# Four small transposes moved from TensorE to VectorE squares and a round trip through HBM

## The chip, the cores and the metric

The kernel runs on one core of a Trainium2 chip. The metric is the device time of one execution in microseconds (us). Before the change it is 1434.01 us, the median of three runs (1433.89 to 1434.04).

The core has a matrix engine (TensorE, PE in the views; PEld is its loading of the stationary operand), a vector engine (VectorE, DVE), a scalar engine (ScalarE, ACT), GpSimd (POOL) and a sync engine (SP), which here only issues transfers. Each engine takes its instructions in the order of its own list and waits, where an operand isn't ready, with everything behind it. SBUF is the on-chip memory of 128 partitions, PSUM holds TensorE's results, HBM is the memory off the core.

## What is computed

Two layers of a gated block with two branches on 512 tokens of width 1024, all in float32. From the reference, cut:

```python
proj = rmsnorm(x, norm1_g[i]) @ w_in[i]
u_pool, q, k, v, g_a, g_b = jnp.split(proj, splits, axis=-1)
q = apply_partial_rotary(rmsnorm(q, q_norm_g[i]), cos, sin)   # 4 heads x 2 parts x 128
k = apply_partial_rotary(rmsnorm(k, k_norm_g[i]), cos, sin)
...
sc = jnp.einsum('bhcqd,bhckd->bhcqk', qi, k) * scale
p = jax.nn.softmax(jnp.where(mask, sc, neg), axis=-1)
a = p[:, :, 0] - lam * p[:, :, 1]
o = jnp.einsum('bhqk,bhkv->bhqv', a, v)
o = rmsnorm(o, subln_g[i]) * (1.0 - lam_init)
merged = jax.nn.sigmoid(g_a) * pool_out + jax.nn.sigmoid(g_b) * attn_out
x = x + merged @ w_out[i]
gate, up = jnp.split(rmsnorm(x, norm2_g[i]) @ w_ffn_in[i], 2, axis=-1)
x = x + (jax.nn.silu(gate) * up) @ w_ffn_out[i]
```

The attention mask lets a block of 128 queries see itself and the blocks before it, so block t has (t + 1) x 128 columns of probabilities.

## The kernel before

**Products.** Every float32 operand is split into a high and a low part (`split`: ScalarE casts the high part, VectorE subtracts for the low one), and a product is three matmuls: high x high, high x low, low x high (lines 279 to 281, and 291 to 294 in the feed-forward part). Weights come in pieces of 512 KB (`piece`): a load on SP's queue into `raw` (7 buffers), then the split into `whi` and `wlo` (6 buffers each). Products are accumulated in PSUM: three buffers `mm`, two `sc`, two `tr` and one `oy`.

**One head** (`attention(j, ...)`, four per layer, heads 3, 2, 1, 0 in this order, with blocks t = 0 to 3 of 128 tokens):

- For each t one product of 8 weight rows gives q and k of the head, 512 columns. ScalarE squares them (line 618), VectorE and GpSimd form the scale r (310, 311), VectorE scales (622) and rotates (`rotate`, 418 to 423) into `qn`.
- `turn(t, qn)`: four TensorE transposes of 128x128 into a `tr` buffer, then the split into `qh` and `ql`.
- `scores(t)`: two products into `sc`, mask, maximum, exponential (560), the two probabilities combined into `pr` (563 to 566).
- `turn_prob(t, pr)`: t + 1 transposes into `tr`, then the split into `ah` and `al`.
- `weighted(t, ah, al)`: the product with v into `oy`, normed and gated into `mt` (588 to 591).
- `turn_out(t, m)`: two transposes, and a copy into `mj` (599).

`merged(j, ...)` later computes the pooled branch of the head with four long products and two short ones and adds `mj`. `project_out` multiplies by w_out. The feed-forward part follows. Layer 0's first head (`at_start`) works on data that was loaded as the kernel began.

**The order of the work.** The program keeps a count of issued matmul columns (`clock`). `later(delay, what)` puts a step in a heap, due `delay` columns from now; before each group of three matmuls `run_due` issues the steps that are due. So QK_WAIT is the number of columns that TensorE is given between the q and k product and their transposes, SCORE_WAIT between those and the scores, PROB_WAIT between scores and the transposes of the probabilities, AV_WAIT between those and the product with v, MERGE_WAIT between that and `turn_out`. `need` runs steps of the heap early where a later part wants them. A scheduler then orders each engine's list by this order and by its own estimate of when operands are ready; each tag of buffers is shared in turn by the tiles that name it (`qn` has three buffers).

Of the kernel before, what the change touches and what calls it, by code (L numbers as in the profile page):

```python
# [43 lines left out]

HIDDEN_AT = {0: "u", 2: "m", 4: "pr", 6: "us", 8: "mj", 10: "u", 12: "m", 14: "pr", 16: "us", 18: "u", 20: "m"}

QK_WAIT, SCORE_WAIT, PROB_WAIT, AV_WAIT, NORM_WAIT, MERGE_WAIT = 20400, 33600, 25200, 11400, 15000, 15000


def weight_plan():  # L50
# [57 lines left out]
def trunk_kernel(  # L108
# [13 lines left out]
    const = ctx.enter_context(tc.tile_pool(name="const", bufs=1))  # L122
    sb = ctx.enter_context(tc.tile_pool(name="sb", bufs=1))
    ps = ctx.enter_context(tc.tile_pool(name="ps", bufs=1, space=PSUM))

    def mm_ps():
        return ps.tile([P, 512], F32, name="mm", tag="mm", bufs=3)
# [171 lines left out]
    def transpose(dst, src):  # L299
        nc.tensor.transpose(dst, src, ident)  # L300
        clock[0] += 2 * P

    def rsqrt_mean(ss, n, width, times=(1.0,), eps=None):

# [120 lines left out]
    def token(t):  # L425
        return slice(t * P, (t + 1) * P)
# [85 lines left out]
            transpose(row[:, token(t)], stats[:, 1, t:t + 1].broadcast_to([P, P]))  # L512
        nc.scalar.copy(rms_row, row)

    later(4 * QK_WAIT, spread_rms)

    for layer in range(L):
        lam_init = 0.8 - 0.6 * math.exp(-0.3 * layer)
# [12 lines left out]
        def attention(j, before, then):  # L531

            if before is not None:
                need(*((layer, before, "s", t) for t in range(NT)))
            qh, ql = pair("q", "qk", 4)
            mj = sb.tile([P, 2, S], F32, name="mj", tag="mj", bufs=2)

            def v_at(v, t):
                return v[:, t // 2, t % 2 * VD:(t % 2 + 1) * VD]

            def turn(t, qn):
                tp = tr_ps()
                for h in range(4):
                    transpose(tp[:, h * P:(h + 1) * P], qn[:, h, :])
                split(qh[:, :, token(t)], ql[:, :, token(t)], tp.rearrange("p (h c) -> p h c", h=4))
                later(SCORE_WAIT, lambda: scores(t))

            def scores(t):
                width = (t + 1) * P
                prob = []  # L550
                st = small("st", 2)
                mx = small("mx", 2)
                for c in range(2):
                    sc = s_ps()
                    product(sc[:, :width], [(
                        (qh[:, c, token(t)], ql[:, c, token(t)]), (qh[:, 2 + c, :width], ql[:, 2 + c, :width]))])
                    nc.vector.memset(sc[:CHUNK, width - CHUNK:width], MASKED)
                    nc.vector.tensor_reduce(mx[:, c:c + 1], sc[:, :width], axis=AX.X, op=ALU.max, negate=True)
                    pr = sb.tile([P, S], F32, name="pr", tag=f"pr{c}", bufs=2)
                    nc.scalar.activation(pr[:, :width], sc[:, :width], AF.Exp, bias=mx[:, c:c + 1], accum_out=st[:, c:c + 1])  # L560
                    prob.append(pr[:, :width])
                rc = small("rc", 2)
                nc.vector.reciprocal(rc, st)
                nc.vector.tensor_mul(rc[:, 1:2], rc[:, 1:2], neglam[layer])
                nc.vector.tensor_scalar_mul(prob[1], prob[1], rc[:, 1:2])
                nc.vector.scalar_tensor_tensor(prob[0], prob[0], rc[:, 0:1], prob[1], op0=ALU.mult, op1=ALU.add)
                later(PROB_WAIT + (4000 if at_start and t == NT - 1 else 0), lambda: turn_prob(t, prob[0]))
                ready.add((layer, j, "s", t))

            def turn_prob(t, pr):  # L570
                tp = tr_ps()
                for k in range(t + 1):
                    transpose(tp[:, token(k)], pr[:, token(k)])
                apart = at_start and t % 2
                ah, al = (sb.tile([P, S], F32R, name="a" + p, tag="u" if apart else "a" + p, bufs=2 if apart else 1) for p in "hl")
                width = (t + 1) * P
                split(ah[:, :width], al[:, :width], tp[:, :width])
                later(AV_WAIT, lambda: weighted(t, ah, al))

            def weighted(t, ah, al):  # L580
                if (layer, j, "v", t) not in ready:
                    later(2400, lambda: weighted(t, ah, al))
                    return
                o = s_ps()[:, :VD] if at_start and t % 2 else o_ps()
                product(o, [((ah[:, token(k)], al[:, token(k)]), (v_at(vh, k), v_at(vl, k))) for k in range(t + 1)])
                ss = small("sso")
                m = sb.tile([P, VD], F32, name="mt", tag="mt", bufs=3)
                nc.scalar.activation(m, o, AF.Square, accum_out=ss)
                r = rsqrt_mean(ss, VD, 1, (1.0 - lam_init,))
                nc.vector.scalar_tensor_tensor(m, o, r, sg[layer], op0=ALU.mult, op1=ALU.mult)  # L590
                nc.vector.scalar_tensor_tensor(m, tb[t // 2][:, t % 2, :], 1.0, m, op0=ALU.add, op1=ALU.mult)
                ready.add((layer, j, "o", t))
                later(MERGE_WAIT, lambda: turn_out(t, m))

            def turn_out(t, m):
                tp = tr_ps()
                for a in range(2):
                    transpose(tp[:, a * P:(a + 1) * P], m[:, a * P:(a + 1) * P])
                nc.scalar.copy(mj[:, :, token(t)], tp[:, :VD].rearrange("p (a c) -> p a c", a=2))
                ready.add((layer, j, "mj", t))  # L600

            at_start = not layer and j == ORDER[0]
            if not at_start:
                w = wblock(KD)
            for t in range(NT):
                if at_start:
                    acc = first_acc[t]
                    first_products(t, steps[2] + steps[3])
                    if not t:
                        token_stats()  # L610
                else:
                    need((f"x{layer}", t))
                    acc = mm_ps()
                    product(acc, list(zip(x_tok(t), w)))
                qn = sb.tile([P, 4, QK], F32, name="qn", tag="qn", bufs=3)
                ss = small("ss4", 4)
                for h in range(4):
                    nc.scalar.activation(qn[:, h, :], acc[:, h * QK:(h + 1) * QK], AF.Square, accum_out=ss[:, h:h + 1])
                r = rsqrt_mean(ss, QK, 4, (QK ** -0.5, 1.0), None if layer else [stats[:, i, t:t + 1] for i in (3, 4)])
                for h in range(4):  # L620
                    g = qkg[layer][:, h // 2 * QK:(h // 2 + 1) * QK]
                    nc.vector.scalar_tensor_tensor(
                        qn[:, h, :], acc[:, h * QK:(h + 1) * QK], r[:, h:h + 1], g, op0=ALU.mult, op1=ALU.mult)
                rotate(qn, t)
                later(17400 + 5700 * t if at_start else QK_WAIT, lambda t=t, qn=qn: turn(t, qn))
                if not t and then is not None:
                    then()
            if before is not None:
                need(*((layer, before, "o", t) for t in range(NT)))
            vh, vl = pair("v", "v", 2)  # L630
            tb = [sb.tile([P, 2, VD], F32, name="tb", tag="tb", bufs=2) for _ in range(2)]
            w = wblock(KD)
            if at_start:
                with tc.issue_after(transfers[-1].ins):
                    for i in range(L):
# [373 lines left out]
```

## Time and profile before

| | |
|---|---|
| median of three runs | 1434.01 us |
| the profiled execution | 1433.82 us, its span 1432.0 us |
| TensorE busy | 1427.0 us, 100% of the span |
| VectorE busy | 990.3 us, 69% |
| ScalarE busy | 687.3 us, 48% |
| TensorE clock granted | 1.00 |
| moved by DMA | 171.97 MB |

The attention parts of the two layers stand at about 30 to 350 us and 735 to 1055 us of the span; the feed-forward parts follow each. A row of instruction groups reads: line, engine, operation, written tile <- read tiles, shapes, count | busy us in total, mean ns of one | idle time of the engine ahead of them and what ended it. Where a view gives three numbers in ns they are the least, the median and the most. A matmul's duration runs from its start to its modelled end; the next one starts before that end.

### The profile page before, as it was taken

What the parts mean: (1) busy time and instruction counts of PE and PEld (TensorE: products, weight loads), DVE (VectorE), ACT (ScalarE), POOL (GpSimd) and SP (SyncE); (2) the same over time, 40 slices, a digit from 0 to 9 for tenths busy, and PEclk for the clock granted to TensorE, in tenths of its full rate; (3) what the DMA queues carried; (4) which work ended last, traced back from release to release, by engine and by line L of the source; (5) the groups of instructions that cost most, each with busy time, mean ns of one, the idle gap of its engine ahead of it and who ended that gap; (6) DMA issues with size and microseconds to landing.
All of it is one profiled execution on the core that took longest, in us unless ns stands there. A gap on an engine that the chain in (4) does not pass through costs nothing.

```text
span 1432.0 us, 21581 instructions
## 1 busy us (share of the span) xinstructions
PE 1427.0 (100%) x8378; PEld 1261.0 (88%) x8378; DVE 990.3 (69%) x1839; ACT 687.3 (48%) x1309; POOL 113.5 (8%) x144
## 2 busy tenths in 40 slices
PE   9999999999999999999999999999999999999999
PEld 7888888888999899989888888888889998999897
DVE  7768677677998548737576686665769975577462
ACT  6544343454667346525354443434547662564350
POOL 1010000100001001000011001001000000010000
PEclk9999999999999999999999999999999999999999
DMA  9212231224268357628331232222323683575361
GB/s 363 97 60 78 93 102 59 89 83 116 74 169 203 115 132 182 187 58 235 105 103 67 62 115 82 74 75 73 123 69 87 169 227 93 141 183 162 88 148 59
DMA packets 49494, 171.97 MB, mean 120 GB/s; under 512 B 5616, under 2 KB 6512, under 8 KB 49392
## 3 DMA queue, kind: packets, MB, share of 16 engines
q1 hardware_dynamic: 39456, 137.02, 28.9%
q0 software_dynamic: 8640, 31.46, 12.4%
q10 hardware_dynamic: 1296, 2.11, 0.5%
q8 instruction: 66, 1.08, 0.3%
q14 instruction: 36, 0.29, 0.1%
HBM read 168.47 MB, written 2.10 MB: 119 GB/s over the span
## 4 chain that ended last, share of the span: by engine, by line
PE 99%; DMA 0%; DVE 0%; ACT 0%; issue 0%
PE mm L279 20%; PE mm L281 20%; PE mm L280 20%; PE mm L293 6%; PE mm L294 6%; PE mm L291 6%; PE sc L291 3%; PE sc L294 3%; PE sc L293 3%; PE tr L300 3%; PE tr L294 1%; PE tr L293 1%; PE tr L291 1%; PE sc L281 1%; PE sc L280 1%; PE sc L279 1%
## 5 line engine op out<-in xcount | busy, mean ns | idle before, releaser
L195 ACT CAST whi<-raw 128x1024 fp32r<-128x1024 f32 (+1 forms) x225 | 234.4, 1048 | 207.6 <-issue 119.0
L196 DVE TENSOR_TENSOR wlo<-raw,whi 128x1024 fp32r<-128x1024 f32 (+1 forms) x225 | 271.6, 1214 | 81.9 <-ACT whi L195 79.0
L279 PE MATMUL mm<-whi,xh 128*128 128x512 f32 x480 | 192.4, 401 | 0.0
L281 PE MATMUL mm<-whi,xl 128*128 128x512 f32 x480 | 187.7, 391 | 0.0
L280 PE MATMUL mm<-wlo,xh 128*128 128x512 f32 x480 | 187.3, 390 | 0.0
L722 DVE TENSOR_TENSOR res<-mm,res 128x512 f32<-128x512 f32 (+1 forms) x97 | 65.8, 682 | 116.0 <-PE mm L281 116.0
L281 PE MATMUL mm<-whi,fl 128*128 128x512 f32 (+1 forms) x358 | 138.5, 387 | 0.0
L279 PE MATMUL mm<-whi,fh 128*128 128x512 f32 (+1 forms) x358 | 138.3, 387 | 0.0
L280 PE MATMUL mm<-wlo,fh 128*128 128x512 f32 (+1 forms) x358 | 138.2, 387 | 0.0
L311 POOL TENSOR_TENSOR r<-r,mhalf 128x1 f32<-128x1 f32 (+1 forms) x76 | 59.1, 778 | 633.3 <-DVE r L310 568.8
L281 PEld LDWEIGHTS mm<-whi,xl 128*128 128x128 f32 x480 | 90.1, 188 | 19.6
L279 PEld LDWEIGHTS mm<-whi,xh 128*128 128x128 f32 x480 | 90.3, 188 | 16.8
L280 PEld LDWEIGHTS mm<-wlo,xh 128*128 128x128 f32 x480 | 90.4, 188 | 16.3
L279 PE MATMUL mm<-xh,whi 128*128 128x512 f32 x256 | 102.1, 399 | 0.0
L235 POOL DMA_DIRECT2D wlo<-in_wts x60 | 52.6, 877 | 612.7 <-ACT wlo L234 271.0
L281 PE MATMUL mm<-xh,wlo 128*128 128x512 f32 x256 | 99.9, 390 | 0.0
L280 PE MATMUL mm<-xl,whi 128*128 128x512 f32 x256 | 99.8, 390 | 0.0
L293 PE MATMUL mm<-xql,whi 128*128 128x256 f32 x352 | 99.7, 283 | 0.0
L294 PE MATMUL mm<-xqh,wlo 128*128 128x256 f32 x352 | 99.6, 283 | 0.0
L291 PE MATMUL mm<-xqh,whi 128*128 128x256 f32 x352 | 99.6, 283 | 0.0
L291 PE MATMUL sc<-xqh,whi 128*128 128x256 f32 x320 | 90.7, 283 | 0.0
L291 PE MATMUL mm<-xrh,whi 128*128 128x256 f32 x320 | 90.6, 283 | 0.0
(235 smaller groups left out, 3533.0 us busy)
## 6 DMA issues: line engine op xcount, KB each, us to landing
raw<-in_wts SPq DMA_DIRECT2D x244, 512.0 KB, 4.3
wlo<-in_wts POOLq DMA_DIRECT2D x60, 512.0 KB, 7.7
xr<-in_x_t SPq DMA_DIRECT2D x4, 512.0 KB, 7.2
res<-in_x SPq DMA_DIRECT2D x4, 512.0 KB, 9.3
pwr<-in_pool_w ACTq DMA_DIRECT2D x8, 256.0 KB, 2.7
out<-res SPq DMA_DIRECT2D x7, 256.0 KB, 2.0
g<-in_gains SPq DMA_DIRECT2D x6, 256.0 KB, 3.2
hg<-in_rows SPq DMA_DIRECT2D x4, 128.0 KB, 6.8
```

The costliest lines, as they stand in the source:

```text
L195: ins = nc.scalar.copy(hi, src)
L196: nc.vector.tensor_sub(lo, src, hi.bitcast(F32))
L235: nc.gpsimd.dma_start(lo.rearrange("p a b -> p (a b)"), wts[piece_no], accum_op=ALU.add)
L279: nc.tensor.matmul(acc, lhsT=ah, rhs=bh, start=i == 0, stop=False)
L280: nc.tensor.matmul(acc, lhsT=ah, rhs=bl, start=False, stop=False)
L281: nc.tensor.matmul(acc, lhsT=al, rhs=bh, start=False, stop=i == n - 1)
L291: nc.tensor.matmul(acc[:, i, :], lhsT=ah, rhs=bh, start=start and not i and not k, stop=False, skip_group_check=True)
L293: nc.tensor.matmul(acc[:, i, :], lhsT=ah, rhs=bl, start=False, stop=False, skip_group_check=True)
L294: last = nc.tensor.matmul(acc[:, i, :], lhsT=al, rhs=bh, start=False, stop=i == 1 and k == 3, skip_group_check=True)
L300: nc.tensor.transpose(dst, src, ident)
L311: nc.gpsimd.tensor_tensor(r, r, mhalf[:, :width], op=ALU.pow)
L722: added = nc.vector.tensor_add(res[t][:, cs], here, res[t][:, cs])
```

## The change

For all heads but the first of layer 0, q, k and the probabilities are no longer transposed by TensorE. A new function `turned` has VectorE transpose each 32x32 square of the tile in place of its column of squares, writes the result to a buffer in HBM and reads it back in four transfers, one for each group of 32 partitions, which put each square into its place. The splits into `qh`, `ql`, `ah`, `al` then read SBUF (`near`) instead of PSUM. The heads' outputs go the same way, except for the first head of layer 0 and the last head of each layer (`near_end`). The delays of these steps get new values: QK_AWAY + SCORE_AWAY equals QK_WAIT + SCORE_WAIT, PROB_AWAY is 6800 columns more than PROB_WAIT, MERGE_AWAY 9000 more than MERGE_WAIT. The buffers `near` share the tags `qn`, `pr0`/`pr1` and `mt`.

```diff
+QK_AWAY, SCORE_AWAY, PROB_AWAY, MERGE_AWAY = 28000, 26000, 32000, 24000
...
+    hbm = ctx.enter_context(tc.tile_pool(name="hbm", bufs=1, space=bass.MemoryType.DRAM))
...
+    def turned(src, n, tag, bufs):
+
+        near = sb.tile([P, n * P], F32, name="near", tag=tag, bufs=bufs)
+        away = hbm.tile([P, n * P], F32, name="away", tag="away", bufs=8)
+        nc.vector.transpose(near.rearrange("p (c k j) -> p k c j", c=4, k=n), src.rearrange("p (k c i) -> p k c i", k=n, c=4))
+        nc.sync.dma_start(away, near)
+        for c in range(4):
+            nc.sync.dma_start(
+                near[32 * c:32 * (c + 1), :].rearrange("i (q r) -> i q r", q=4),
+                away.rearrange("(q i) (c r) -> c i q r", q=4, c=4)[c])
+        return near.rearrange("p (q k j) -> p k q j", q=4, k=n)
...
             def turn(t, qn):
-                tp = tr_ps()
-                for h in range(4):
-                    transpose(tp[:, h * P:(h + 1) * P], qn[:, h, :])
-                split(qh[:, :, token(t)], ql[:, :, token(t)], tp.rearrange("p (h c) -> p h c", h=4))
-                later(SCORE_WAIT, lambda: scores(t))
+                if at_start:
...
+                else:
+                    split(squares_of(qh[:, :, token(t)]), squares_of(ql[:, :, token(t)]), qn)
+                later(SCORE_WAIT if at_start else SCORE_AWAY, lambda: scores(t))
...
+                if at_start:
+                    later(PROB_WAIT + (4000 if t == NT - 1 else 0), lambda: turn_prob(t, prob[0]))
+                else:
+                    near = turned(prob[0], t + 1, f"pr{t % 2}", 2)
+                    later(PROB_AWAY, lambda: turn_prob(t, near))
...
-                later(MERGE_WAIT, lambda: turn_out(t, m))
+                if near_end:
+                    later(MERGE_WAIT, lambda: turn_out(t, m))
+                else:
+                    near = turned(m, 2, "mt", 3)
+                    later(MERGE_AWAY, lambda: turn_out(t, near))
...
             at_start = not layer and j == ORDER[0]
+            near_end = at_start or j == ORDER[-1]
...
-                later(17400 + 5700 * t if at_start else QK_WAIT, lambda t=t, qn=qn: turn(t, qn))
+                if not at_start:
+                    qn = turned(qn.rearrange("p h c -> p (h c)"), 4, "qn", 3)
+                later(17400 + 5700 * t if at_start else QK_AWAY, lambda t=t, qn=qn: turn(t, qn))
```

How the change moves the lists of the engines is shown at two places. The first is SP's list in layer 0's attention. Before, behind the loads of x into `res`, one row of 48 weight loads (`raw<-in_wts`) goes on to the feed-forward part:

```order
L209 DMA raw<-in_wts 128x1024 x48
```

After, the same weight loads stand between stores (`away<-near`) and loads (`near<-away`) of the round trips; this is a stretch in the third head, where outputs of the second (128x256), then q and k (128x512) and the first probabilities (128x128) are sent:

```order
L311 DMA away<-near 128x256
L212 DMA raw<-in_wts 128x1024 x2
L313 DMA near<-away 32x4x64 x4
L311 DMA away<-near 128x512
L313 DMA near<-away 32x4x128 x4
L212 DMA raw<-in_wts 128x1024 x2
L311 DMA away<-near 128x512
L313 DMA near<-away 32x4x128 x4
L212 DMA raw<-in_wts 128x1024
L311 DMA away<-near 128x512
```

Each `near<-away` stands behind its own store, which it waits for, and the weight loads behind it wait with it.

The second place is VectorE's list in the same head, at the scores of its first block: the end of the softmax (`rc`, `pr`), the scaling of the last block's q and k (`qn`), a weight split (`wlo`). Before:

```order
L558 TENSOR_REDUCE mx<-sc 128x1
L196 TENSOR_TENSOR ql<-tr,qh 128x4x128
L196 TENSOR_TENSOR wlo<-raw,whi 128x1024
L563 RECIPROCAL rc<-st 128x2
L310 TENSOR_SCALAR r<-ss_1853,stats 128x2
L564 TENSOR_TENSOR rc<-rc,nl_71 128x1
L310 TENSOR_SCALAR r<-ss_1853,stats 128x2
L565 TENSOR_SCALAR pr<-pr,rc 128x128
L622 SCALAR_TENSOR_TENSOR qn<-mm,r,hg 128x128
L566 SCALAR_TENSOR_TENSOR pr<-pr,rc 128x128
L622 SCALAR_TENSOR_TENSOR qn<-mm,r,hg 128x128 x3
L196 TENSOR_TENSOR wlo<-raw,whi 128x1024
```

After, from the reciprocal on:

```order
L584 RECIPROCAL rc<-st 128x2
L328 TENSOR_SCALAR r<-ss_1925,stats 128x2
L585 TENSOR_TENSOR rc<-rc,nl_73 128x1
L328 TENSOR_SCALAR r<-ss_1925,stats 128x2
L586 TENSOR_SCALAR pr<-pr,rc 128x128
L199 TENSOR_TENSOR ql<-near,qh 128x4x128
L587 SCALAR_TENSOR_TENSOR pr<-pr,rc 128x128
L659 SCALAR_TENSOR_TENSOR qn<-mm,r,hg 128x128
L310 STREAM_TRANSPOSE near<-pr 128x128
L659 SCALAR_TENSOR_TENSOR qn<-mm,r,hg 128x128 x3
L199 TENSOR_TENSOR wlo<-raw,whi 128x1024
```

The low part of q and k (`ql`), which read PSUM and stood ahead of the reciprocal, now reads `near` and stands between the two last steps of `pr`; behind them is the new square transpose of `pr`. The `ql` is that of the second block, whose own square transpose stands eighteen rows further up.

More of the change, by code (lines that the diff above doesn't have):

```diff
@@ L45 @@
 HIDDEN_AT = {0: "u", 2: "m", 4: "pr", 6: "us", 8: "mj", 10: "u", 12: "m", 14: "pr", 16: "us", 18: "u", 20: "m"}
-QK_WAIT, SCORE_WAIT, PROB_WAIT, AV_WAIT, NORM_WAIT, MERGE_WAIT = 20400, 33600, 25200, 11400, 15000, 15000
+SCORE_WAIT, PROB_WAIT, AV_WAIT, NORM_WAIT, MERGE_WAIT = 33600, 25200, 11400, 15000, 15000
+QK_AWAY, SCORE_AWAY, PROB_AWAY, MERGE_AWAY = 28000, 26000, 32000, 24000
 def weight_plan():
@@ L301, in transpose, with squares_of @@
         clock[0] += 2 * P
+    def turned(src, n, tag, bufs):
[8 more added lines that the diff above has]
+        return near.rearrange("p (q k j) -> p k q j", q=4, k=n)
+    def squares_of(x):
+        return x.rearrange("p k (q j) -> p k q j", q=4)
     def rsqrt_mean(ss, n, width, times=(1.0,), eps=None):
@@ L513, in spread_rms @@
         nc.scalar.copy(rms_row, row)
-    later(4 * QK_WAIT, spread_rms)
+    later(81600, spread_rms)
     for layer in range(L):
@@ L541, in turn @@
             def turn(t, qn):
-                tp = tr_ps()
-                for h in range(4):
-                    transpose(tp[:, h * P:(h + 1) * P], qn[:, h, :])
-                split(qh[:, :, token(t)], ql[:, :, token(t)], tp.rearrange("p (h c) -> p h c", h=4))
-                later(SCORE_WAIT, lambda: scores(t))
+                if at_start:
+                    tp = tr_ps()
+                    for h in range(4):
+                        transpose(tp[:, h * P:(h + 1) * P], qn[:, h, :])
+                    split(qh[:, :, token(t)], ql[:, :, token(t)], tp.rearrange("p (h c) -> p h c", h=4))
+                else:
+                    split(squares_of(qh[:, :, token(t)]), squares_of(ql[:, :, token(t)]), qn)
+                later(SCORE_WAIT if at_start else SCORE_AWAY, lambda: scores(t))
             def scores(t):
@@ L566, in scores @@
                 nc.vector.scalar_tensor_tensor(prob[0], prob[0], rc[:, 0:1], prob[1], op0=ALU.mult, op1=ALU.add)
-                later(PROB_WAIT + (4000 if at_start and t == NT - 1 else 0), lambda: turn_prob(t, prob[0]))
+                if at_start:
[3 more added lines that the diff above has]
+                    later(PROB_AWAY, lambda: turn_prob(t, near))
                 ready.add((layer, j, "s", t))
             def turn_prob(t, pr):
-                tp = tr_ps()
-                for k in range(t + 1):
-                    transpose(tp[:, token(k)], pr[:, token(k)])
+                if at_start:
+                    tp = tr_ps()
+                    for k in range(t + 1):
+                        transpose(tp[:, token(k)], pr[:, token(k)])
                 apart = at_start and t % 2
@@ L576, in turn_prob @@
                 width = (t + 1) * P
-                split(ah[:, :width], al[:, :width], tp[:, :width])
+                if at_start:
+                    split(ah[:, :width], al[:, :width], tp[:, :width])
+                else:
+                    split(*(squares_of(x[:, :width].rearrange("p (k c) -> p k c", c=P)) for x in (ah, al)), pr)
                 later(AV_WAIT, lambda: weighted(t, ah, al))
@@ L592, in weighted @@
                 ready.add((layer, j, "o", t))
-                later(MERGE_WAIT, lambda: turn_out(t, m))
-            def turn_out(t, m):
[L596 to L599, printed above, removed]
+                if near_end:
+                    later(MERGE_WAIT, lambda: turn_out(t, m))
+                else:
+                    near = turned(m, 2, "mt", 3)
+                    later(MERGE_AWAY, lambda: turn_out(t, near))
+            def turn_out(t, m):
+                if near_end:
+                    tp = tr_ps()
+                    for a in range(2):
+                        transpose(tp[:, a * P:(a + 1) * P], m[:, a * P:(a + 1) * P])
+                    nc.scalar.copy(mj[:, :, token(t)], tp[:, :VD].rearrange("p (a c) -> p a c", a=2))
+                else:
+                    nc.scalar.copy(squares_of(mj[:, :, token(t)]), m)
                 ready.add((layer, j, "mj", t))
             at_start = not layer and j == ORDER[0]
+            near_end = at_start or j == ORDER[-1]
             if not at_start:
```

## Prediction

> **What bounds the kernel now.** I read the totals of the page and its chain first, then who TensorE waited for, then the transposes.
>
> ```profile
> span 1432.0 us, 21581 instructions
> ...
> PE 1427.0 (100%) x8378; PEld 1261.0 (88%) x8378; DVE 990.3 (69%) x1839; ACT 687.3 (48%) x1309; POOL 113.5 (8%) x144
> ...
> PE 99%; DMA 0%; DVE 0%; ACT 0%; issue 0%
> ```
> ```profile
> PE mm L438 <- DVE cold L431: 1.2, 1, 1.2
> PE tr L494 <- DVE xh L481: 0.3, 1, 0.3
> ```
> TensorE is busy for the whole span and is 99% of the chain that ended last. The second view is the complete list of what it waited for: 1.5 us, all in the first microseconds. So every instruction taken from TensorE shortens the run by its place in that chain, and every wait added to TensorE lengthens it. All else is a question of whether something new makes TensorE wait. The profiled execution took 1433.82 us around the span of 1432.0 us, against a median of 1434.01 us. I calculate from 1433.8.
>
> **What is removed.** By line 300, the transposes and their sources (min/median/max ns):
>
> ```profile
> L300 PE MATMUL tr<-ident,qn x128: 270/272/297, 29.2 to 989.6; 128*128 128x128 f32 x128
> L300 PE MATMUL tr<-ident,pr x80: 270/272/273, 55.8 to 1018.8; 128*128 128x128 f32 x80
> L300 PE MATMUL tr<-ident,mt x64: 270/271/275, 69.5 to 1033.2; 128*128 128x128 f32 x64
> ```
> There are 8 heads (4 in each of 2 layers). A head has 16 transposes of q and k, 10 of probabilities, 8 of outputs. Seven heads lose the first two kinds, five lose the third: 7 x 16 + 7 x 10 + 5 x 8 = 112 + 70 + 40 = 222. The diff fixes that count, so I see no way for the change to miss its object.
>
> The 270 ns are not what a transpose costs, since matmuls overlap. The chain (start, us, what) and the timeline (start, us, instruction) show the step from one to the next:
>
> ```profile
> 180.34 0.23 PE mm L280
> 180.57 0.23 PE mm L281
> 180.80 0.44 PE tr L300 x4
> 181.24 0.23 PE mm L279
> ```
> ```profile
> 122.54 0.39 PE L281 MATMUL mm<-xh,wlo 128*128 128x512 f32 x1
> 122.77 0.38 PE L300 MATMUL tr<-ident,mt 128*128 128x128 f32 x2
> 122.91 0.48 PE L279 MATMUL mm<-xh,whi 128*128 128x512 f32 x1
> 123.22 0.39 PE L280 MATMUL mm<-xl,whi 128*128 128x512 f32 x1
> ```
> Four transposes hold the chain 0.44 us, 0.11 each. For a pair: from L281 at 122.54 to L280 at 123.22 is 0.68 us, of which two ordinary steps are 2 x 0.23 = 0.45, so the pair took 0.23, or 0.115 each. q and k: 112 x 0.11 = 12.3. Probabilities, in groups of one to four: 70 x 0.112 = 7.9. Outputs: 40 x 0.115 = 4.6. **Removed from TensorE: 24.8 us.** With no new wait the run takes 1433.8 - 24.8 = 1409.0 us.
>
> **What is added on VectorE.** Of each removed group one 32x32-square transpose of the same width: 28 of 512 columns, 7 each of 128, 256, 384 and 512, 20 of 256. The trace has no such operation. Its nearest rows, f32 on VectorE, and the widest and cheapest rows beside them (busy us, mean ns):
>
> ```profile
> L196 DVE TENSOR_TENSOR ul<-us,uh 128x512 fp32r<-128x512 f32 x16 | 11.1, 692 | 9.5 <-ACT uh L195 9.5
> L196 DVE TENSOR_TENSOR al<-tr,ah 128x384 fp32r<-128x384 f32 x8 | 4.4, 555 | 6.6 <-ACT ah L195 6.6
> L196 DVE TENSOR_TENSOR fl<-th,fh 128x256 fp32r<-128x256 f32 x88 | 32.9, 416 | 0.2
> L196 DVE TENSOR_TENSOR al<-tr,ah 128x128 fp32r<-128x128 f32 x8 | 2.3, 289 | 5.6 <-ACT ah L195 5.6
> L565 DVE TENSOR_SCALAR pr<-pr,rc 128x512 f32<-128x512 f32 x8 | 3.9, 484 | 0.2
> L196 DVE TENSOR_TENSOR wlo<-raw,whi 128x1024 fp32r<-128x1024 f32 x223 | 270.2, 1219 | 78.1 <-ACT whi L195 75.2
> ```
> I take one element a cycle, as the rows that process two f32 inputs show: 28 x 0.69 + 7 x (0.69 + 0.56 + 0.42 + 0.29) + 20 x 0.42 = 19.3 + 13.7 + 8.4 = 41.4 us. Were it as cheap as L565, about 0.7 of that, 29 us; were each element passed twice, as the 1024-column row, 1.77 of that, 73 us. Busy time in the two stretches of attention, in columns PE, PEld, DVE, ACT, POOL, then clock, DMA share and GB/s:
>
> ```profile
> 30.00:350.00 320.00, 320.00 (x1559) 267.63 (x1558) 227.21 (x565) 141.43 (x362) 25.38 (x32) 1.00 0.27 90
> 735.00:1055.00 320.00, 320.00 (x1558) 267.97 (x1557) 211.93 (x531) 141.35 (x370) 23.16 (x30) 1.00 0.26 84
> ```
> VectorE is busy 439.1 of 640 us and idle 200.9. 41 us fit, and 73 would. The splits into high and low part now read SBUF instead of PSUM. That costs ScalarE some 35 ns each (621 against 586 ns for 512 columns, rows below) in an engine with 357 us free there, and VectorE 10 ns (692 above against 682). I count both as nothing.
>
> ```profile
> L195 ACT CAST qh<-tr 128x512 fp32r<-128x512 f32 x32 | 18.7, 586 | 22.0 <-PE tr L300 21.9
> L195 ACT CAST uh<-us 128x512 fp32r<-128x512 f32 x16 | 9.9, 621 | 56.1 <-DVE us L675 43.1 <-DVE us L682 12.9
> ```
>
> **What is added in transfers.** 76 stores and 304 loads go on SP's queue, among the weight loads. The rows on that queue: issue time of one, landing times, and its longest wait (total us, times, longest):
>
> ```profile
> L209 SPq DMA_DIRECT2D raw<-in_wts x152: 327/328/373, 8.8 to 1379.3; - x152
> ```
> ```profile
> raw<-in_wts SPq DMA_DIRECT2D x244, 512.0 KB, 4.3
> ...
> out<-res SPq DMA_DIRECT2D x7, 256.0 KB, 2.0
> ```
> ```profile
> SPq L209 <- DVE wlo L196: 492.0, 98, 21.6
> ```
> A round trip is a store (0.33 issue, about 2.0 to land), then four loads (4 x 0.33, the last landing about 2.0 later): 5.7 us at best. Each leg may stand behind one weight transfer of 512 KB; with 4.3 in place of 2.0 on one leg it is 8.0, on both 10.3. I take 6 to 9. SP is held by a round trip until its loads are issued: 0.33 + 2.0 + 1.3 = 3.6 us, 76 x 3.6 = 274, and the weight issues of these stretches, at most 152 x 0.33 = 50. So SP is held about half of the 640 us, and its 492 us of waiting for VectorE's splits show that weight loads are limited by buffers, not by issue. This hides the hold; the cover ends where stores take some 6 us to land ((640 - 50)/76 = 7.8 a trip).
>
> By the Trainium skill (DMA: Bandwidth & Descriptors, Specifications), transfers reach line rate from 512 bytes up and below that do a read-modify-write. The loads of narrow probabilities and of outputs move runs of 128 to 384 bytes; no run here shows that price, and doubling their time would still sit inside 10.3.
>
> **Whether anything reaches TensorE late.** Its order is set by columns issued, 512 of them in 0.227 us. Before, q and k wait 20400 + 33600 columns from product to score; after, 28000 + 26000: the same 54000, or 23.9 us. The rows of the work on them:
>
> ```profile
> L618 ACT ACTIVATE qn<-mm 128x128 f32<-128x128 f32 x112 | 29.5, 281 | 34.3 <-PE mm L281 34.3
> L618 ACT ACTIVATION_READ_ACCUMULATOR qn<-mm 128x1 f32 x112 | 23.6, 211 | 0.0
> L622 DVE SCALAR_TENSOR_TENSOR qn<-mm,r,hg 128x128 f32<-128x128 f32 x112 | 31.9, 344 | 29.3 <-POOL r L311 29.3
> L311 POOL TENSOR_TENSOR r<-r,mhalf 128x1 f32<-128x1 f32 (+1 forms) x76 | 59.1, 778 | 633.3 <-DVE r L310 568.8
> ```
> 4 x 0.49 for the squares, 0.8 for the power, 4 x 0.34 for the scaling, and by estimate 1.5 for the six small VectorE steps between (r, rotation) are 5.6 us. With 0.7 for the square transpose, a trip of 6 to 9 and 1.3 for the two splits that is 14 to 17 us. Probabilities get 32000 + 11400 = 43400 columns, 19.2 us, where they had 36600. Their longest path in the trace, the first block of a later head:
>
> ```profile
> 173.86 0.28 PE L281 MATMUL sc<-qh,ql 128*128 128x128 f32 x1
> ```
> ```profile
> 181.73 0.34 DVE L566 SCALAR_TENSOR_TENSOR pr<-pr,rc 128x128 f32<-128x128 f32 x1
> ```
> They are done 8.1 us after the scores end (173.98). Then 0.3 for the transpose, the trip, 0.6 for the splits: 15 to 18 of 19.2. Outputs are wanted only after four more products of 5.4 us. So on average all comes in time, but for probabilities with 1 to 4 us to spare, and VectorE works in order: where a split waits for a late load, what stands behind it waits too. The engine order in the text ahead shows such a place: ql stands before the last step of pr and the scaling of qn. VectorE's own rows between that square transpose and ql add to about 9 us, as long as the slow end of a trip. I therefore allow TensorE **4 us of new waits** in all, out of 56 such splits: between 0 (every trip under 9 us) and 8 (some fifteen places half a microsecond late). Sum: 1409.0 + 4.0 = **1413.0 us**, and 1409 to 1417 as its own range.
>
> **Rivals.** (a) *Late landings at VectorE.* Trips of 9 to 11 us, behind weight transfers on both legs: many of the 56 splits hold VectorE a microsecond or two, qn and weight splits behind them come late, and TensorE waits 8 to 22 us: 1417 to 1431. For it: the order above, and that the DMA share, 0.27, is in bursts. Against it: accumulators and weight pieces are several deep.
>
> (b) *Slower: VectorE becomes the bound.* After the 41 us it has 160 us free in attention. Split over 56 splits, that is 2.9 us each; beyond a trip of about 9 + 2.9 = 12 us its waits exceed what is free and pass to TensorE. At 13 us a trip the price is 56 x (4.0 - 2.9) = 62 us: 1409 + 62 = 1471. For it: raw's landing of 4.3 us on a lightly loaded queue. Against it: 12 us need both legs slower than two ordinary weight landings.
> The Trainium skill (VectorE: DVE Perf Modes, Rules for kernel authors) says to transpose 128x128 on TensorE where PSUM will do as the target, which it did here; that rule speaks for this rival, and the trace bears it out only in that the step was cheap, 0.11 us.
>
> (c) *Same.* The waits of (a) eat 22 to 28 of the 24.8 us: 1431 to 1437.
>
> (d) *More than the chain step is gained*, if each group also hid a hand-over on TensorE's queue: with 0.12 in place of 0.112 us, 222 x 0.008 = 2 us, 1407.
>
> **How the numbers follow.** Forecast 1409 to 1417: 0.57. (a) 0.20. (b) 0.13. (c) 0.07. (d) 0.03. A measurement of this kernel can tell about 0.2%, 2.9 us. Faster: 0.57 + 0.20 + 0.03 = 0.80; same 0.07; slower 0.13. The range must reach over (a) to leave out no more than 0.2: 1407 to 1431.
>
> **What would show it.** Right: TensorE 99% of the chain, 222 fewer of the 128-column transposes, its list of waits only a few us longer; VectorE about 41 us busier; a square transpose of 512 columns near 0.7 us; trips of 6 to 9 us. Wrong in the waits: ScalarE's qh and ah, or VectorE behind them, waiting on near for tens of us, and TensorE on al, ql, vl, wlo or mm. Wrong in the price: square transposes above 1.2 us. Wrong in SP's hold: weight casts waiting for raw.

## The result, and the profile after

The changed kernel takes **1411.17 us** (median of six runs, 1411.06 to 1411.68) against 1434.03 us before, a ratio of 0.984 (95% interval 0.983 to 0.985): 22.9 us gained. Its profiled execution took 1411.17 us around a span of 1409.4 us.

The page of the changed kernel, span, busy times and the chain that ended last by engine:

```profile
span 1409.4 us, 21870 instructions
...
PE 1403.4 (100%) x8156; PEld 1239.0 (88%) x8156; DVE 1023.0 (73%) x1915; ACT 686.8 (49%) x1309; POOL 118.2 (8%) x144
...
PE 95%; DVE 2%; DMA 1%; issue 0%; POOL 0%; ACT 0%; SPq 0%; DVEq 0%; POOLq 0%; ACTq 0%
```

TensorE is still the bound, with 8378 - 8156 = 222 instructions fewer, and its busy time fell by 23.6 us. In 3% of the span the chain now leaves it for VectorE and the transfers, which it did not before. The rows of TensorE's transposes by line 303 (ns: least, median, most) show which are left:

```profile
L303 PE MATMUL tr<-ident,mt x24: 270/272/273, 69.8 to 1014.7; 128*128 128x128 f32 x24
L303 PE MATMUL tr<-ident,qn x16: 270/272/273, 29.4 to 45.5; 128*128 128x128 f32 x16
L303 PE MATMUL tr<-ident,pr x10: 270/271/273, 56.0 to 71.7; 128*128 128x128 f32 x10
```

In their place stand VectorE's square transposes, by line 310:

```profile
L310 DVE STREAM_TRANSPOSE near<-qn x28: 699/711/715, 70.3 to 968.0; 128x512 f32<-128x512 f32 x28
L310 DVE STREAM_TRANSPOSE near<-pr x28: 299/508/711, 96.6 to 990.9; 128x128 f32<-128x128 f32 x7, 128x256 f32<-128x256 f32 x7, 128x384 f32<-128x384 f32 x7, 128x512 f32<-128x512 f32 x7
L310 DVE STREAM_TRANSPOSE near<-mt x20: 404/439/447, 114.1 to 924.8; 128x256 f32<-128x256 f32 x20
```

What TensorE waits for in the changed kernel (engine, instruction <- what ended the wait: us in total, times, longest), the whole list, and then the two rows of the weight loads that feed the product with v:

```profile
PE mm L456 <- DVE cold L449: 1.2, 1, 1.2
PE oy L284 <- DVE al L199: 0.5, 2, 0.4
PE tr L512 <- DVE xh L499: 0.4, 1, 0.4
PE oy L282 <- ACT ah L198: 0.2, 1, 0.2
```
```profile
PEld oy L284 <- DVE al L199: 3.2, 7, 0.6
...
PEld oy L282 <- ACT ah L198: 1.2, 3, 0.7
```

The first and third row were there before. New are the waits of the product with v for the two parts of the probabilities, `ah` and `al`: ten weight loads waited 4.4 us, of which the matmul ahead of each covers a part, and the list of the matmuls themselves names only 0.7, since it counts only time in which no matmul was running. No matmul waits for `ql`, `qh`, `vl` or a weight. Busy time in the two stretches of attention (columns as in the prediction):

```profile
30.00:340.00 310.00, 309.23 (x1461) 257.66 (x1461) 240.29 (x595) 141.87 (x361) 27.47 (x31) 1.00 0.43 132
720.00:1035.00 315.00, 314.68 (x1469) 262.31 (x1468) 235.86 (x588) 144.59 (x381) 26.01 (x31) 1.00 0.45 139
```

VectorE is busy 476 of 625 us. Before, TensorE was busy for 640.0 of 640 us; now 1.1 us are missing, and the DMA share has gone from 0.27 to 0.44.

### The profile page after: what moved, and what is told of

Read it like the earlier page. It is cut to its first block, busy times and chain, and to the rows that moved or that the text cites. A ratio compares the mean times of both kernels' runs of the same rounds, so it can differ in the third digit from the quotient of the medians.

```text
span 1409.4 us, 21870 instructions
## 1 busy us (share of the span) xinstructions
PE 1403.4 (100%) x8156; PEld 1239.0 (88%) x8156; DVE 1023.0 (73%) x1915; ACT 686.8 (49%) x1309; POOL 118.2 (8%) x144
## 3 DMA queue, kind: packets, MB, share of 16 engines
q0 software_dynamic: 8640, 31.46, 12.6%
## 4 chain that ended last, share of the span: by engine, by line
PE 95%; DVE 2%; DMA 1%; issue 0%; POOL 0%; ACT 0%; SPq 0%; DVEq 0%; POOLq 0%; ACTq 0%
PE mm L282 19%; PE mm L284 19%; PE mm L283 19%; PE mm L296 6%; PE mm L297 6%; PE mm L294 6%; PE sc L294 3%; PE sc L297 3%; PE sc L296 3%; PE tr L297 1%; PE tr L296 1%; PE tr L294 1%; PE tr L303 1%; PE sc L284 1%; PE sc L283 1%; PE sc L282 1%
## 5 line engine op out<-in xcount | busy, mean ns | idle before, releaser
L282 PE MATMUL mm<-whi,xh 128*128 128x512 f32 x480 | 188.7, 393 | 0.0
L329 POOL TENSOR_TENSOR r<-r,mhalf 128x1 f32<-128x1 f32 (+1 forms) x76 | 63.8, 840 | 614.5 <-DVE r L328 493.5
```

The costliest lines, as they stand in the source:

```text
L282: nc.tensor.matmul(acc, lhsT=ah, rhs=bh, start=i == 0, stop=False)
L329: nc.gpsimd.tensor_tensor(r, r, mhalf[:, :width], op=ALU.pow)
```

## Experiments

All were timed against the kernel before on the same chip (its medians lay between 1433.94 and 1434.07 us) and are told as edits of the changed kernel.

### Each kind alone

`qk_only` moves q and k alone; probabilities (here and in `turn_prob`) and outputs stay on TensorE:

```diff
-                if at_start:
-                    later(PROB_WAIT + (4000 if t == NT - 1 else 0), lambda: turn_prob(t, prob[0]))
+                if True:
+                    later(PROB_WAIT + (4000 if at_start and t == NT - 1 else 0), lambda: turn_prob(t, prob[0]))
...
-            near_end = at_start or j == ORDER[-1]
+            near_end = True
```

`prob_only` moves the probabilities alone; q and k go back to TensorE in `turn` and at the place below, and `near_end = True` as above. `out_only` combines this edit with that of the probabilities and keeps `near_end` as the change has it.

```diff
-                if not at_start:
-                    qn = turned(qn.rearrange("p h c -> p (h c)"), 4, "qn", 3)
-                later(17400 + 5700 * t if at_start else QK_AWAY, lambda t=t, qn=qn: turn(t, qn))
+                later(17400 + 5700 * t if at_start else QK_WAIT, lambda t=t, qn=qn: turn(t, qn))
```

> Only q and k go through squares and HBM; probabilities and outputs are transposed by TensorE as before. Theory (each removed transpose is worth its step in the chain, 0.11 us): 112 x 0.11 = 12.3 us less than 1434.0, and no new wait: 1421.7 (1421 to 1423). Rival (a transpose is worth its own duration of 0.27 us, and new waits eat the rest): 30 us less, less waits, and a list of waits of 5 us or more.

> Only the probabilities go through squares and HBM, with the delay of 32000 columns. Theory: 70 x 0.112 = 7.9 us less than 1434.0, and up to 2.2 us of waits for ah and al: 1426.1 to 1428.3. Rival (the waits belong to the crowd on VectorE and SP that q, k and the outputs make): 1426.1 with no waits for ah and al.

> Only the five heads' outputs go through squares and HBM. Theory: 40 x 0.115 = 4.6 us less than 1434.0, no new wait: 1429.4 (1429 to 1430). Rival (0.27 us each): 1423.2.

| moved | median us | ratio (95% interval) | gained | per transpose |
|---|---|---|---|---|
| q, k (112) | 1421.37 | 0.991 (0.990 to 0.993) | 12.6 | 0.112 |
| probabilities (70) | 1425.90 | 0.994 (0.993 to 0.996) | 8.0 | 0.115 |
| outputs (40) | 1428.92 | 0.996 (0.995 to 0.998) | 5.1 | 0.128 |
| all | 1411.17 | 0.984 (0.983 to 0.985) | 22.9 | 0.103 |

Each kind alone gains the whole of its transposes. The three sum to 25.7 us, and together they bring 22.9: **2.8 us are lost between them**. The probabilities are the part whose data I had thought tight, but alone they cost no wait. TensorE's whole list in `prob_only`:

```profile
PE mm L456 <- DVE cold L449: 1.2, 1, 1.2
PE tr L512 <- DVE xh L499: 0.2, 1, 0.2
PE mm L282 <- ACT mh L204: 0.2, 1, 0.2
```

So the round trip by itself is not late at 43400 columns. What makes it late comes with the other parts.

### In pairs

`qk_prob` sets `near_end = True` (outputs on TensorE), `prob_out` leaves q and k there.

> q, k and probabilities through squares and HBM, all outputs transposed by TensorE. The parts alone gained 12.6 and 8.0 us, without a wait for ah or al; all three together gained 22.8 and not 25.7. Theory (the outputs' trips, which run while the probabilities' trips run, make these late): no interplay here, 1413.4 within 0.5 and no waits for ah and al. Rival (q's and k's trips make them late): the missing 2.9 us are here, 1415.5 to 1416.3.

> Probabilities and outputs through squares and HBM, q and k transposed by TensorE. The parts alone gained 8.0 and 5.1 us. Theory (the outputs' trips make the probabilities late): the interplay is here, 1434.0 - 13.1 + 2 to 2.9 = 1423 to 1423.8, with waits for ah and al. Rival (q's and k's trips do it, or it takes all three): 1420.9 within 0.5 without such waits.

`qk_prob` took 1414.09 us, ratio 0.986 (0.985 to 0.988); by the sum of its parts it would take 1413.4. `prob_out` took 1421.47, ratio 0.991 (0.990 to 0.993), against 1420.9. Each pair loses 0.6 or 0.7 us, near what these medians can tell from nothing: a little more than the 0.5 that I had allowed for no interplay, and far from the 2 to 2.9 us of the other answer. TensorE's list names one wait for `al` in `qk_prob`, 0.5 us, and none in `prob_out`. Neither of these pairs holds the 2.8 us. The third pair, q and k with outputs, was not run, so that it takes all three is likely but not shown.

### What it is that comes late

In the changed kernel, around 826 us, TensorE runs one ordinary step of 0.23 us and then stands until 826.54 (start, us, instruction):

```profile
826.02 0.40 PE L282 MATMUL mm<-xh,whi 128*128 128x512 f32 x1
826.54 0.38 PE L284 MATMUL oy<-vh,al 128*128 128x256 f32 x1
```

It waited for `al`. ScalarE had cast the high part of the same tile two microseconds earlier, so all its columns were back from HBM (the last of its four loads had landed at 819.26):

```profile
824.06 0.51 ACT L198 CAST ah<-near 128x384 fp32r<-128x384 f32 x1
```

VectorE's timeline for that time:

```profile
824.36 0.68 DVE L199 TENSOR_TENSOR ul<-us,uh 128x512 fp32r<-128x512 f32 x1
824.96 0.44 DVE L310 STREAM_TRANSPOSE near<-mt 128x256 f32<-128x256 f32 x1
825.34 0.67 DVE L715 TENSOR_TENSOR us<-us 128x512 f32<-128x512 f32 x1
...
825.93 0.55 DVE L199 TENSOR_TENSOR al<-near,ah 128x384 fp32r<-128x384 f32 x1
```

Its input complete since 824.57, `al` stands behind a split of the pooled branch, the square transpose of an **output** and a sum of the pooled branch. VectorE isn't waiting here, it is working through its list. The wait is one of order in the engines' lists, not of the trip: after the landing ScalarE's list took 4.8 us to reach the cast, and VectorE's another 1.4 to reach `al`. The 28 low parts of probabilities each have a time between their end and the first matmul that reads them; 0.06 us means that TensorE was waiting. From the starts and durations in the trace:

| | at most 0.1 us | median us | probabilities' delay |
|---|---|---|---|
| after | 7 of 28 | 2.2 | 32000 |
| prob_25 | 11 | 0.3 | 25200 |
| prob_38 | 3 | 4.3 | 38000 |

All seven places of the changed kernel are of this kind. The last load had landed 0.2 to 6.7 us before ScalarE began the cast, `al` began 0.5 to 3.9 us after the cast had ended, and VectorE was not idle just ahead of it.

How much time is lost there can be counted from the starts of the matmuls. A step is the time from one start to the next. Taken over all steps that end at a product with v from 90 us on, this is how far they exceed the median step between the same shapes in the kernel before (us in total):

| before | qk_only | prob_only | out_only | qk_prob | prob_out | after | prob_25 | prob_38 | last_out | best |
|---|---|---|---|---|---|---|---|---|---|---|
| 0.3 | 0.7 | -0.2 | 0.3 | 0.8 | 0.0 | 3.1 | 6.1 | 2.7 | 3.2 | 0.4 |

The changed kernel stands 2.8 us above the kernel before, and each part alone at most 0.3: the missing 2.8 us are at the products with v. (The last four runs follow below.)

### The delay of the probabilities

`prob_38` has a longer delay; `prob_25` has 25200 in the same place, the value of the kernel before.

```diff
-QK_AWAY, SCORE_AWAY, PROB_AWAY, MERGE_AWAY = 28000, 26000, 32000, 24000
+QK_AWAY, SCORE_AWAY, PROB_AWAY, MERGE_AWAY = 28000, 26000, 38000, 24000
```

> Only the delay between scores and the split of the returned probabilities is longer: 38000 columns for 32000, 2.7 us. Theory (the 2.2 us that are missing from 24.8 are TensorE's waits for ah and al, because the probabilities come back a little late): those waits vanish from TensorE's list and the time falls by about 2 us, from 1411.2 to 1409.2 (1408.7 to 1409.9). Rival (the missing 2 us are VectorE's fuller list, or removed transposes that were worth 0.10 and not 0.112 us): the time stays at 1411.2 within 0.5.

> The same delay shorter: 25200 columns, the value it had with TensorE's transposes, 3.0 us less than 32000. Theory (deadline of the probabilities): nine of the 28 returns came with nothing to spare and ten more with 1 to 3 us, so every head now waits some 3 us at its products with v: 7 x 3 = 21 us, 1432 (1422 to 1442), that is, nothing left of the gain. Rival (trips hidden, waits come from elsewhere): 1411 to 1413.

`prob_38` took 1410.79 us, ratio 0.984 (0.983 to 0.985): 0.4 us better, where I had looked for two. Most of the waits for `al` and `ah` went, but a new one came (the longest in its list):

```profile
PE oy L282 <- DVE mt L619: 1.7, 1, 1.7
```

It falls in layer 1's first head. The last block's product with v starts at 781.93, right after VectorE has read the block before it out of `oy` (L619, 781.30 to 781.78). That reading came late by other engines' lists: ScalarE had squared the block by 776.75, VectorE's next step for it began at 779.38, and GpSimd's then took from 779.67 to 781.27. The two products stand 7.8 us apart, against 5.2 in the changed kernel, so it isn't that one follows too closely on the other, as I took it to be for `best` below. So several short waits were traded for a long one.

`prob_25` took 1415.91 us, ratio 0.988 (0.986 to 0.989), 4.7 us worse than 32000. The direction was right, the size was not: I had expected some 21 us. Its profiled execution was 4.0 us longer than that of the changed kernel: by the count of steps 3.0 of them stand at the products with v and 0.5 at the scores. The two rows that answer to those of the changed kernel:

```profile
PEld oy L284 <- DVE al L199: 4.6, 10, 1.5
PEld oy L282 <- ACT ah L198: 4.0, 9, 0.9
```

The due time moved by 6800 columns, 3.0 us, and the median time to spare by 1.9; in eleven places nothing was left. My reading, which no run tests by itself: a wait of TensorE moves all that stands behind it back, the next deadline too, which is then met. I had priced each place as if the others had not waited.

### VectorE's share doubled

```diff
         nc.vector.transpose(near.rearrange(...), src.rearrange(...))
+        nc.vector.transpose(near.rearrange(...), src.rearrange(...))
         nc.sync.dma_start(away, near)
```

> Each square transpose is made twice on VectorE, into the same place, so that VectorE is busier by another 42 us or so and nothing else changes. Theory (VectorE has room, only the returning probabilities are late): each trip starts 0.3 to 0.7 us later, so the waits for ah and al grow from 2 to some 5 us: 1412 to 1417. Rival (VectorE is about to be the bound): 1425 or more, with TensorE waiting on mm, wlo or vl.

1419.95 us (1418.70 to 1420.66), ratio 0.990 (0.989 to 0.991): 8.8 us for another 43 us of VectorE's time, between what the two theories gave. TensorE's waits, the two largest, and the busy time of both stretches:

```profile
PE oy L284 <- DVE al L199: 2.8, 3, 1.6
PE sc L283 <- DVE ql L199: 1.8, 1, 1.8
```
```profile
30.00:345.00 315.00, 313.42 (x1477) 259.95 (x1476) 256.15 (x633) 141.87 (x362) 26.85 (x32) 1.00 0.42 132
725.00:1045.00 320.00, 314.82 (x1458) 260.87 (x1457) 251.18 (x623) 142.57 (x374) 26.28 (x31) 0.99 0.44 138
```

VectorE is busy 80% of these stretches and has 128 us free, yet TensorE stands in some places for want of `al` and `ql`. A list with time free on average is late where several steps come together. That fits a crowd at some places, and not the engine's whole capacity. Each trip also starts later here, by 0.3 to 0.7 us, and the run can't tell this from the fuller list.

### The trip doubled

```diff
+        again = hbm.tile([P, n * P], F32, name="again", tag="again", bufs=8)
+        nc.sync.dma_start(again, near)
+        nc.sync.dma_start(near, again)
         return near.rearrange("p (q k j) -> p k q j", q=4, k=n)
```

> Behind the four loads the tile is stored once more and loaded back as it is, which adds some 5 us to each trip. Theory (deadlines, not capacity): every head waits for its probabilities 3 to 6 us and for some q and k: 7 x 5 = 35 us, 1446 (1435 to 1460), with TensorE's list of waits naming ah, al, qh and ql. Rival (the prediction's case b, VectorE becomes the bound at 12 us a trip): 1471, VectorE over nine tenths busy or waiting on ScalarE in attention and TensorE waiting on wlo and mm. Rival (trips are hidden): under 1415.

1442.30 us (1438.99 to 1446.29), ratio 1.006 (1.005 to 1.007): 31 us worse than the change, and slower than the kernel before. The largest waits, and the busy time:

```profile
PE sc L282 <- ACT qh L198: 7.7, 5, 2.7
PE mm L283 <- DVE wlo L199: 3.2, 1, 3.2
PE oy L284 <- DVE al L199: 2.4, 3, 0.9
```
```profile
30.00:340.00 310.00, 304.07 (x1411) 249.36 (x1410) 233.31 (x588) 135.37 (x353) 25.80 (x30) 0.99 0.55 170
740.00:1065.00 325.00, 312.53 (x1423) 253.39 (x1422) 228.79 (x568) 138.60 (x365) 25.94 (x30) 0.99 0.59 185
```

Now q and k are late too. This is the slower case that I had weighed, and it came by another way. The trips grew by more than the 5 us that I expected: from the end of a square transpose of probabilities to the cast that reads the result the median is 17.6 us (13.6 to 29.0), against 8.5 in the changed kernel, so they are beyond the 13 us of that case. VectorE's share is 73% of these 635 us, against 76% in the changed kernel, and over the whole run it waited some 25 us at the splits of returned tiles, where that case has it wait for more than the 160 us that it has free. Its capacity was not used up: operands missed their deadlines. By estimate 6.6 of the 31 us are a lower clock (last section).

### Two versions beyond the change

`last_out` is `prob_38` with the outputs of the last heads sent through HBM as well, 16 transposes more:

```diff
-QK_AWAY, SCORE_AWAY, PROB_AWAY, MERGE_AWAY = 28000, 26000, 32000, 24000
+QK_AWAY, SCORE_AWAY, PROB_AWAY, MERGE_AWAY = 28000, 26000, 38000, 24000
-            near_end = at_start or j == ORDER[-1]
+            near_end = at_start
```

`best` adds to it that layer 1's first head keeps the delay of 32000, to be rid of the wait for `oy`:

```diff
-                    later(PROB_AWAY, lambda: turn_prob(t, near))
+                    later(32000 if layer and j == ORDER[0] else PROB_AWAY, lambda: turn_prob(t, near))
```

> The delay of prob_38, and also the outputs of the last head of each layer go through squares and HBM, 16 transposes fewer. Theory: 16 x 0.115 = 1.8 us less than prob_38 if the outputs are back before the last merge wants them, 1407.4. Rival (there they are wanted at once): the last merge and w_out wait some 3 us in each layer, 1409 to 1416.

> last_out, but with the delay of 32000 columns kept in layer 1's first head, where 38000 columns put the last product with v right behind the one ahead of it and TensorE waited 1.84 us for a free half of oy. Theory: that wait goes and the gain of the longer delay in the other heads stays: 1408.9 - 1.8 = 1407.1 (1406.8 to 1408). Rival (the wait there comes from how close the two heads follow each other, whatever the delay): 1408.5 to 1409.

`last_out`: 1408.94 us, ratio 0.983 (0.981 to 0.984), 1.85 us below `prob_38`, 0.116 for each of the 16. (The 1407.4 started from the 1409.2 that I had looked for in `prob_38`, and missed by as much.) `best`: **1406.15 us** (1406.13 to 1406.65), ratio 0.981 (0.979 to 0.982), 27.9 us below the kernel before, 5.0 below the change and a little below the range that I expected. What TensorE waits for in it, the whole list, and the first stretch:

```profile
PE mm L456 <- DVE cold L449: 1.2, 1, 1.2
PE tr L512 <- DVE xh L499: 0.3, 1, 0.3
PE oy L284 <- DVE al L199: 0.2, 1, 0.2
```
```profile
30.00:340.00 310.00, 310.00 (x1465) 259.33 (x1464) 243.37 (x603) 142.91 (x362) 28.27 (x32) 1.00 0.43 137
```

The list is that of the kernel before, but for 0.2 us, and TensorE is busy 310.00 of 310 us again. 238 transposes at the 25.7/222 = 0.116 us that the three parts showed would be 27.6, and 27.9 came: the 2.8 us were these waits, since without them nothing is missing. The count of steps agrees, 0.4 us at the products with v for 3.1 in the changed kernel. (It also finds most of the last step, from `last_out` to `best`: 2.7 us, where the rows for `mt` in `last_out` name 1.7 and 0.3.)

## Why the prediction was right, and where its steps were off

1. **"Removed from TensorE: 24.8 us", at 0.11 us a transpose.** Right in kind, 0.9 us too small: 25.7 by the three parts alone. q and k gave 12.6 for 12.3, probabilities 8.0 for 7.9, outputs 5.1 for 4.6. The last is off by 11%; I took it from a pair of transposes between two long matmuls. But that half microsecond isn't firm: executions of one kernel differ by as much (1428.85 to 1429.23 here, 1433.86 to 1434.75 for the kernel before beside it). Case (d), a gain per transpose above the chain's step, came in part at most, at 0.116 and not 0.12, and no run shows its hidden hand-over.
2. **"I allow TensorE 4 us of new waits."** 2.8 us by the difference above. Both deviations go the same way, 0.9 and 1.2, and less the 0.2 by which I started too low (1433.8 for 1434.03) they make, but for rounding, the 1.8 us between 1413.0 and 1411.2. That the allowance came near is in part luck, since the way in which I had the waits arise (3) did not occur.
3. **Where the waits come.** I named the probabilities as the tight part, "with 1 to 4 us to spare", and VectorE's list as what would make them late. Both hold: waits for `al` and `ah` only, median to spare 2.2 us, and the one shown in full was late by VectorE's list. My picture of how was wrong. I expected a split that waits for a late load and holds up what stands behind it. VectorE's waits at these splits fell, from 21.8 us in the kernel before to 10.5 (before, then after):

```profile
DVE al L196 <- ACT ah L195: 12.2, 11, 1.6
DVE ql L196 <- ACT qh L195: 9.6, 7, 2.6
```
```profile
DVE ql L199 <- ACT qh L198: 9.0, 9, 2.6
DVE al L199 <- ACT ah L198: 1.5, 3, 0.8
```

   In the seven places with nothing to spare the loads were back, and the split stood in a queue of ready work, on ScalarE and then on VectorE. ScalarE's queue, on an engine with 357 us free, I did not price at all. That the two pairs show little of the loss agrees with this, since each part adds to those queues.
4. **VectorE's price.** 0.71 us for 512 columns against 0.69 taken, so the rows with two f32 inputs were the right measure. 28 x 0.71 + 28 x 0.5 + 20 x 0.44 = 43 us for 41.4 predicted. The engine's busy time rose by only 32.7, because it counts records that overlap once: the durations of all its instructions add up to 1080.7 us before and 1125.4 after, 44.7 more.
5. **The trip.** From the end of a square transpose of probabilities to the cast that reads the result: median 8.5 us of 28, from 6.5 to 14.7, four above 13; 18 of 28 are at most 9, the upper end that I took. This holds ScalarE's own queue too: to the landing of the last load it is 4.8 to 9.8 us, median 7.4. (The work ahead of the trip I had 0.2 us too long: in the row shown the scores end at 174.14, not 173.98.) Most landing times (KB each, median us) are close to the 2.0 that I had from ordinary transfers:

```profile
away<-near SPq DMA_DIRECT2D x35, 256.0 KB, 2.4
near<-away SPq DMA_DIRECT2D x140, 64.0 KB, 2.1
near<-away SPq DMA_DIRECT2D x28, 48.0 KB, 3.3
near<-away SPq DMA_DIRECT2D x108, 32.0 KB, 2.3
```

   The three rows of loads move runs of 512, 384 and 256 bytes; those of 128 bytes (16 KB) took 2.1. So no price that grows as the runs get shorter can be seen. Why the 384-byte loads took 3.3 us stays open, as do the 3.2 us of the smallest stores (64 KB).

6. **SP's hold.** I counted 3.6 us from a store's issue to the last load's. SP's waits in the changed kernel show a hold that I had left out, before the store:

```profile
SPq L212 <- DVE wlo L199: 217.0, 69, 17.1
SPq L311 <- DVE near L310: 124.8, 46, 8.7
SPq L313 <- DMA away<-near: 50.9, 35, 3.2
```

   It stood 124.8 us for VectorE's squares and 50.9 for its own stores, and issuing the 304 loads took 130 us, where I had counted 100. The cover held: its wait for weight buffers, 492.0 before, fell to 217.0, and no weight came late. It is more than half used.

7. **The rivals.** (a) at 1417 to 1431 and (c) at 1431 to 1437 did not come; TensorE's waits were an eighth to a third of the 8 to 22 us of (a). (b) did not come at this length of trip. `two_trips` shows that a longer trip does end slower than before, but at 1442 with trips of some 17 us, not the 1471 that I worked out for 13, and neither VectorE's busy time nor its waits at the splits used up its room: that mechanism is refuted here. The Trainium skill (VectorE: DVE Perf Modes, Rules for kernel authors) would have left these transposes on TensorE; here they cost 0.116 us each of the bound there, and on VectorE, which had room, only the 2.8 us of waits that they made, and the measurement decides.

## What to carry to other kernels

On the engine that is the bound, price an instruction by the step that it takes in the chain, not by its duration (0.116 us against 0.270), and it is worth moving off even where it then costs more elsewhere (a group of four: 0.44 us of TensorE, or 0.71 us of VectorE and some 8 us of trip), so long as every result has a deadline that the trip meets. Test the parts alone and together: here each was free by itself, the two pairs that were run lost little, and the loss came with all three in the same ordered lists. A returned tile can be late though its transfer isn't: look at where its steps stand in each engine's list. Of the delays that were run, the shorter one cost less than the places that it made late suggest, and the longer one brought a new wait at the end of one head; no single value served all heads best.

## What was not expected of the hardware

**Half the clock after a pause.** In `two_trips` TensorE stood twice within four microseconds, and its granted clock then fell (columns as above; the clock is the third number from the end):

```profile
264.00:266.00 2.00, 0.72 (x3) 0.41 (x3) 2.00 (x6) 1.78 (x3) 0.00 (x0) 1.00 0.45 131
266.00:268.00 2.00, 0.79 (x6) 0.75 (x7) 2.00 (x7) 0.00 (x0) 0.00 (x0) 1.00 0.45 123
268.00:270.00 2.00, 2.00 (x6) 1.51 (x5) 1.99 (x7) 1.04 (x2) 0.00 (x0) 0.53 0.65 184
270.00:272.00 2.00, 2.00 (x7) 1.62 (x6) 2.00 (x3) 1.75 (x13) 0.00 (x0) 0.62 0.89 250
```

Matmuls there take a step of 0.43 us in place of 0.23, from 268.1 to 271.5, at a granted clock of 0.50. `two_trips` has four such stretches, from 107.7, 268.1, 766.5 and 862.0 us, each 3.41 us long. TensorE was busy 13.2 us in them; by estimate half of that, 6.6 us, is what they cost. In `dve_twice` one followed the single pause of 1.8 us before `ql` (from 809.1, 3.41 us at 0.50); in `prob_38`, after its pause of 1.7 us, the clock stayed at 1.00. So a wait of about two microseconds can cost nearly as much again, and not each time. The Trainium skill (TensorE: Matmul & The Clock Gate, Part 1: The HAM clock gate) tells of a free-running window of about 3.4 us and half the rate after at least one idle window. The length of the slow time agrees, and so does the free running: the four stretches begin whole multiples of 3.413 us apart (47, 146 and 28 of them). That the window must be idle does not: in the 3.41 us ahead of the four TensorE was busy 1.8, 1.6, 0.7 and 0.5 us.

**Issue on SP.** A load of the trip took SP 302 to 2247 ns to issue, median 429, where a weight load before took 327 to 373.
